# Issuing the rope's row swaps from ScalarE into a tile of their own, in a fused hybrid decoder block

## The chip, the cores and the metric

The kernel runs on one core of a Trainium2 chip. The metric is the device time of one launch in microseconds (us). An engine is named as in the profile: PE is TensorE (PEld its weight loads), DVE is VectorE, ACT is ScalarE, POOL is GpSimd, SP is SyncE, whose queue issues nearly all DMAs.

## The reference, cut to what matters

One decoder layer over 2048 tokens of 1024 channels: an adaptive RMSNorm, one input projection into queries (8 heads of 64), keys and values (2 heads) and a gated convolution group, sliding-window attention with rotary positions, an output projection, a gated MLP of 2816 channels with a convolution, and a last RMSNorm, all in float32. The changed part is the rotary step (rope):

```python
def rope(x, positions):
    ...
    x1, x2 = xf[..., :half], xf[..., half:]
    out = jnp.concatenate([x1 * cos - x2 * sin, x2 * cos + x1 * sin], axis=-1)
    return out.astype(x.dtype)
...
q = rope(q.reshape(bsz, s, N_Q_HEADS, HEAD_DIM), positions)
k = rope(k.reshape(bsz, s, N_KV_HEADS, HEAD_DIM), positions)
```

Each half of a head (32 channels) needs the other half of the same head.

## The kernel before, in words

Channels lie on partitions and tokens along the free axis. The mixer (the first 850 us or so) goes through four quarters q = 0 to 3 of 512 tokens. In a quarter the projection is computed in steps of one 128-channel tile: 24 matmuls of 128x512 into a PSUM tile `ps`, of which there are two. For q > 0 the order is k (tile 4), q0, q1, v (tile 5), and then, as filler between attention pieces, q2, q3 and the twelve convolution tiles. The attention goes in eight pieces g (4 blocks of 128 tokens for each key head): `scores(g)` (matmuls `sc<-kt,qs`), softmax, `trans(g)` (transposes into `tr`, then the copies `pt`), `pv(g)`. scores(0) to scores(3) need the roped k, q0 and q1; later ones need q2 and q3. Each scores(g) has two halves: the first reads the `qs` tile of q0 (or q2), the second that of q1 (or q3). scores(0) stands after q2 and two eighths of q3 in quarters 1 to 3, and inside the second convolution tile in quarter 0, where the six tiles of k, q and v are done in `start` with PSUM banks of their own.

A roped tile comes about so: ACT copies `ps` to `rq` with a bias (L496, `evac_bias`); four DMAs of 32x512 (64 KB) from SP, L503, copy `rq` into a tile `sq` with the two 32-row halves of each head exchanged; DVE multiplies `rq` by the cosines `cs[:, 0]` (L504) and `sq` by the signed sines `cs[:, 1]` (L505) and adds them into `rq` (L506); ACT copies halves of `rq` to the rounded high parts (L337 and L534, into `kt` for k, four copies, or `qs` for q, two), and DVE takes the low parts (L338, L535). L504 writes `rq`, which the four DMAs read, so it waits for the last of them.

The tile `sq` has two buffers. They also hold the squares of the norm statistics (L323 and L324, one for each of the eight `xr` rows that end the quarter before), so a swap waits until the squares that were there have been added up. The order on each engine is made by a scheduler that plays the program through with a timeline of its own; matmuls keep the order in which they are written. Around the rope in quarters 1 to 3 the eight rows of the last quarter's output are finished: SP loads `xr` (L694), DVE adds to it (L695), SP stores it (L696), ACT squares it (L323).

Of the kernel before, what the change touches and what calls it, by code (L numbers as in the profile page):

```python
# [49 lines left out]
def body(tc, *a):  # L50
    nc = tc.nc
    with tc.tile_pool(name="cst", bufs=1) as cst, \
         tc.tile_pool(name="ps", bufs=1, space=PSUM) as pp, \
         tc.tile_pool(name="dr", bufs=1, space=DRAM) as dr:
        build(nc, tc, cst, pp, dr, *a)


def build(nc, tc, cst, pp, dr, xT, pos, pk_d, c_d, ada_d, w_in, w_o, w_up, w_dn, outT):
# [3 lines left out]
    dma = nc.sync.dma_start  # L62
# [18 lines left out]
    def aux_tile():  # L81
# [2 lines left out]

    TAGS = {'h': (1024, 8), 'y': (1024, 8), 'qs': (1024, 4), 'pp': (1024, 2), 'pt': (512, 6),
# [3 lines left out]

    where = {}  # L90
# [8 lines left out]
    def t(tag, shape=None, dt=F32):  # L99
        p, (n, bufs) = where[tag]  # L100
        return p.tile(shape or [128, n], dt, tag=tag, name=tag, bufs=bufs)
# [396 lines left out]

    def rope(raw, cs, mode=0):
        m = [pool if mode >> i & 1 else vec for i in range(3)]  # L500
        sw = t('sq')
        for i in range(4):
            dma(sw[32 * i:32 * i + 32], raw[32 * (i ^ 1):32 * (i ^ 1) + 32])  # L503
        m[0].tensor_tensor(out=raw, in0=raw, in1=cs[:, 0], op=ALU.mult)  # L504
        m[1].tensor_tensor(out=sw, in0=sw, in1=cs[:, 1], op=ALU.mult)  # L505
        m[2].tensor_tensor(out=raw, in0=raw, in1=sw, op=ALU.add)  # L506
        return raw
# [5 lines left out]
    class Attn:  # L513
# [14 lines left out]
        def k_out(self, p):  # L528
            kr = rope(evac_bias(p, 4, 'rq'), self.cs, RK[self.q])
            kt = self.kt = t('kt', [128, 2, 2, 640], F32R)  # L530
            for kv in range(2):
                own, oth = lohi[kv], lohi[1 - kv]
                split(kt[own, kv, 0, 128:640], kt[own, kv, 1, 128:640], kr[own], vec)
                act(kt[oth, kv, 0, 128:640], kr[own], AF.Copy)  # L534
                vec.tensor_tensor(out=kt[oth, kv, 1, 128:640], in0=kr[own], in1=kt[own, kv, 0, 128:640].bitcast(F32),  # L535
                                  op=ALU.subtract)
            if self.q > 0:
                fdma(kt[:, :, :, 0:128], prev_k[0])
            if self.q < NQ - 1:
                prev_k[0] = sb.tile([128, 2, 2, 128], F32R, tag="hk", name="hk")  # L540
                fdma(prev_k[0], kt[:, :, :, 512:640])

        def q_out(self, j):
            def f(p):
                qr = rope(evac_bias(p, j, 'rq'), self.cs, RQ[self.q][j])
                qt = self.qs[j] = t('qs', [128, 2, 512], F32R)
                for hh in range(2):
                    own, oth = lohi[hh], lohi[1 - hh]
                    split(qt[own, hh], qt[oth, hh], qr[own], pool if SQ[self.q][j] else vec)
            return f  # L550
# [759 lines left out]
```

## Time and profile before

| what | value |
|---|---|
| median of 3 runs | 2240.99 us (2240.96 to 2241.58) |
| profiled execution | 2238.82 us, span 2237.0 us |
| PE, DVE, ACT, POOL busy | 92%, 71%, 44%, 24% of the span |
| mean granted clock of PE | 0.967 of full speed |

The span is that of the program's instructions; the execution is 1.8 us longer than it, and the median 2.2 us longer than the profiled execution.

### The profile page before, as it was taken

Reading aid. Unit: us, or ns where it says so; the run is one execution under the profiler, and the core shown is the slowest. Engines: PE = TensorE matmul, PEld = TensorE weight load, DVE = VectorE, ACT = ScalarE, POOL = GpSimd, SP = SyncE. Lnnn points to the kernel's source line nnn. Section 1 sums busy time; section 2 is a strip of 40 time slices with the busy share of each in tenths; the row PEclk is TensorE's granted clock in tenths of the full one; section 3 lists DMA queues with packets and bytes.
Section 4 is the critical chain, followed back from the end, with each engine's and each line's share of the span. In section 5 each row is a group of like instructions: output and inputs, shape, how many; then the busy total and the mean of one; then the engine's idle time right before and its main releaser. Section 6 shows DMA issues by size and latency. Waiting matters only on the chain.

```text
span 2237.0 us, 26087 instructions
## 1 busy us (share of the span) xinstructions
PE 2058.7 (92%) x8914; PEld 1646.0 (74%) x8914; DVE 1592.7 (71%) x2589; ACT 985.9 (44%) x1719; POOL 532.9 (24%) x306
## 2 busy tenths in 40 slices
PE   4877968988998997999999998999999999999996
PEld 3765757766777775877887877787788888878874
DVE  8897548747854759888888868758877777654454
ACT  3564435435533534544444434544544444434341
POOL 5264410000000001323323323423232323212220
PEclk7998989999999998999999999999999999999997
DMA  7674776677667556545345566665433232256662
GB/s 284 208 257 144 268 252 244 231 255 249 213 215 241 171 177 228 181 149 178 138 172 171 188 202 191 195 198 178 156 104 109 90 112 100 99 175 201 190 203 97
DMA packets 164918, 414.80 MB, mean 185 GB/s; under 512 B 19248, under 2 KB 23344, under 8 KB 152240
## 3 DMA queue, kind: packets, MB, share of 16 engines
q1 hardware_dynamic: 164640, 413.02, 54.5%
q8 instruction: 70, 1.15, 0.2%
q14 instruction: 64, 0.52, 0.1%
q10 hardware_dynamic: 144, 0.11, 0.0%
HBM read 304.52 MB, written 100.93 MB: 181 GB/s over the span
## 4 chain that ended last, share of the span: by engine, by line
PE 44%; DVE 4%; DMA 3%; issue 1%; ACT 1%; SPq 0%; POOL 0%; DVEq 0%; ACTq 0%; POOLq 0%
PE ps L67 21%; PE sc L67 12%; PE tr L67 7%; PE aux L67 2%; PE pv L67 1%; DVE op L338 1%; DMA wr<-tt 1%; DVE S L759 1%; DMA u<-x1d 0%; DMA wr<-w_dn 0%; ACT op L337 0%; DMA tb<-x1d 0%; DMA y<-x1d 0%; DVE x L1118 0%; DMA f<-u 0%
## 5 line engine op out<-in xcount | busy, mean ns | idle before, releaser
L338 POOL TENSOR_TENSOR op<-wr,op 128x512 fp32r<-128x512 f32 (+1 forms) x123 | 240.3, 1954 | 1221.6 <-DVE o L338 585.9
L67 PE MATMUL ps<-h,w 128*128 128x512 f32 x1632 | 425.6, 411 | 37.1 <-ACT rq L496 15.1
L67 PE MATMUL ps<-S,op 128*128 128x512 f32 x1584 | 389.9, 399 | 21.8 <-ACT op L337 11.5
L67 PEld LDWEIGHTS ps<-h,w 128*128 128x128 f32 x1632 | 311.3, 195 | 115.6 <-ACT rq L496 17.7
L67 PEld LDWEIGHTS ps<-S,op 128*128 128x128 f32 x1584 | 299.1, 189 | 98.8 <-ACT op L337 14.7
L337 ACT ACTIVATE op<-wr 128x1024 fp32r<-128x1024 f32 (+1 forms) x229 | 205.1, 896 | 254.6 <-PE sc L67 85.2
L338 DVE TENSOR_TENSOR op<-wr,op 128x1024 fp32r<-128x1024 f32 x106 | 140.4, 1327 | 135.8 <-ACT op L337 135.8
L1007 DVE SCALAR_TENSOR_TENSOR u<-G,pk,u 128x512 f32<-128x512 f32 x176 | 156.5, 891 | 34.2 <-ACT u L1004 32.6
L67 PE MATMUL sc<-S,op 128*128 128x512 f32 x528 | 131.0, 397 | 0.0
L67 PE MATMUL ps<-S,o 128*128 128x512 f32 x528 | 130.4, 395 | 0.0
L67 PE MATMUL tr<-S,op 128*128 128x512 f32 x528 | 130.3, 395 | 0.0
L67 PE MATMUL sc<-S,o 128*128 128x512 f32 x528 | 130.3, 395 | 0.0
L67 PE MATMUL ps<-op 128*128 128x512 f32 x462 | 120.0, 394 | 9.1 <-DVE op L338 4.8
L67 PE MATMUL sc<-op 128*128 128x512 f32 x462 | 118.4, 392 | 0.0
L67 PEld LDWEIGHTS sc<-S,op 128*128 128x128 f32 x528 | 99.8, 189 | 24.3
L67 PEld LDWEIGHTS sc<-S,o 128*128 128x128 f32 x528 | 99.1, 188 | 24.1
L67 PEld LDWEIGHTS tr<-S,op 128*128 128x128 f32 x528 | 99.1, 188 | 24.1
L67 PEld LDWEIGHTS ps<-S,o 128*128 128x128 f32 x528 | 99.0, 188 | 24.0
L67 PEld LDWEIGHTS ps<-op 128*128 128x128 f32 x462 | 86.6, 188 | 29.5 <-DVE op L338 5.6
L1004 ACT ACTIVATE u<-G,pk 128x512 f32<-128x512 f32 x88 | 71.4, 812 | 82.4 <-DVE G L988 80.7
L338 POOL TENSOR_TENSOR w<-wr,w 128x1024 fp32r<-128x1024 f32 x28 | 74.3, 2662 | 137.3 <-ACT w L337 116.3
L337 ACT ACTIVATE op<-ta 128x512 fp32r<-128x512 f32 x132 | 81.0, 624 | 57.6 <-PE ps L67 51.8
(315 smaller groups left out, 3533.6 us busy)
## 6 DMA issues: line engine op xcount, KB each, us to landing
w<-wd SPq DMA_DIRECT2D x72, 1024.0 KB, 5.9
wr<-w_up SPq DMA_DIRECT2D x86, 512.0 KB, 3.3
wd<-w SPq DMA_DIRECT2D x26, 1024.0 KB, 5.4
fs<-u SPq DMA_DIRECT2D x88, 256.0 KB, 2.1
wr<-fs SPq DMA_DIRECT2D x88, 256.0 KB, 2.9
wr<-tt SPq DMA_DIRECT2D x88, 256.0 KB, 3.3
f<-u SPq DMA_DIRECT2D x66, 256.0 KB, 2.0
wr<-f SPq DMA_DIRECT2D x66, 256.0 KB, 2.9
```

The lines of the kernel that those rows point to most:

```text
L67: i = nc.tensor.matmul(*a, **k)
L337: act(hi, src, AF.Copy)
L338: return lo_eng.tensor_tensor(out=lo, in0=src, in1=hi.bitcast(F32), op=ALU.subtract)
L759: vec.scalar_tensor_tensor(out=o[:, L], in0=src, scalar=bias, in1=o[:, W].bitcast(F32), op0=ALU.add, op1=ALU.subtract)
L1004: act(u, G[:, 2:], AF.Identity, scale=fwh[:, 2 * NFF + j:2 * NFF + j + 1], bias=fwh[:, 3 * NFF + j:3 * NFF + j + 1])
L1007: vec.scalar_tensor_tensor(out=u, in0=G[:, i:i + T], scalar=fwh[:, i * NFF + j:i * NFF + j + 1], in1=u, op0=ALU.mult, op1=ALU.add)
```

## The change

Three lines differ. The swapped halves go to a new tile `sw` with one buffer, not to one of the two buffers of `sq`, and the four DMAs are issued by ACT's queue, not by SP's.

```diff
-            'rq': (512, 5), 'hb': (512, 1), 'cv': (512, 2), 'cz': (514, 2), 'xr': (512, 2),
+            'rq': (512, 5), 'hb': (512, 1), 'sw': (512, 1), 'cv': (512, 2), 'cz': (514, 2), 'xr': (512, 2),
...
     def rope(raw, cs, mode=0):
...
-        sw = t('sq')
+        sw = t('sw')
         for i in range(4):
-            dma(sw[32 * i:32 * i + 32], raw[32 * (i ^ 1):32 * (i ^ 1) + 32])
+            nc.scalar.dma_start(sw[32 * i:32 * i + 32], raw[32 * (i ^ 1):32 * (i ^ 1) + 32])
```

There are 20 ropes (five in each quarter), so 80 DMAs change their queue. The order of PE's instructions stays as it was, and so do its PSUM banks; the scheduler reorders the others, mostly within the mixer.

On ACT, at the start of quarter 1, the rows before are these (`rq_2102` is k, `rq_2155` q0, `rq_2201` q1, `rq_2247` v, `rq_2280` q2):

```order
L496 ACTIVATE rq_2102<-ps_2077,pk_69 128x512
L337 ACTIVATE w_2218<-wr_2216 128x1024
L323 ACTIVATE sq_1982<-xr_1978 128x512
L496 ACTIVATE rq_2155<-ps_2130,pk_69 128x512
L337 ACTIVATE w_2251<-wr_2249 128x1024
L323 ACTIVATE sq_2051<-xr_2047 128x512
L496 ACTIVATE rq_2201<-ps_2176,pk_69 128x512
L337 ACTIVATE w_2297<-wr_2295 128x1024
L496 ACTIVATE rq_2247<-ps_2222,pk_69 128x512
L323 ACTIVATE sq_2058<-xr_2054 128x512
L496 ACTIVATE rq_2280<-ps_2255,pk_69 128x512
L337 ACTIVATE kt_2112<-rq_2102 64x512
```

With the change the same place on ACT reads so, from the copy of q0 on:

```order
L496 ACTIVATE rq_2155<-ps_2130,pk_69 128x512
L337 ACTIVATE w_2251<-wr_2249 128x1024
L323 ACTIVATE sq_2051<-xr_2047 128x512
L337 ACTIVATE kt_2112<-rq_2102 64x512
L534 ACTIVATE kt_2112<-rq_2102 64x512
L337 ACTIVATE kt_2112<-rq_2102 64x512
L534 ACTIVATE kt_2112<-rq_2102 64x512
L503 DMA sw_2157<-rq_2155 32x512 x4
L496 ACTIVATE rq_2201<-ps_2176,pk_69 128x512
L337 ACTIVATE w_2297<-wr_2295 128x1024
L496 ACTIVATE rq_2247<-ps_2222,pk_69 128x512
L323 ACTIVATE sq_2058<-xr_2054 128x512
```

The copies of k, which stood behind all five evacuations, now stand ahead of that of q1, with the four issues of q0's swap behind them; after these rows come the copies of q0, then the swap of q1, the evacuation of q2, the copies of q1 and the swap of q2. On DVE, L506 of k stands behind L695 of the seventh `xr` row and L506 of q0 behind L695 of the eighth.

On ACT in quarter 0, ahead of the first exponentials, these rows now stand (`rq_573` is q1, `rq_590` is q2):

```order
L337 ACTIVATE qs_568<-rq_558 64x512 x2
L503 DMA sw_575<-rq_573 32x512 x4
L337 ACTIVATE w_854<-wr_852 128x1024
L496 ACTIVATE cv_771<-ps_746,pk_69 128x512
L337 ACTIVATE w_968<-wr_966 128x1024
L337 ACTIVATE qs_583<-rq_573 64x512 x2
L503 DMA sw_592<-rq_590 32x512 x4
L596 ACT_TABLE_LOAD
```

Before, the copies of all four q tiles stood ahead of `cv_771`, and `w_968` behind the exponentials. On DVE in quarter 0 the rope of q1 now reads so (`sc_791` is the first half of scores(0)):

```order
L504 TENSOR_TENSOR rq_573<-rq_573,cs_523 128x512
L505 TENSOR_TENSOR sw_575<-sw_575,cs_523 128x512
L274 TENSOR_TENSOR g1_104<-g1_104,pk_69 128x2
L589 ISA pp_786,mx_787<-sc_791,mask_88 128x128
L589 ISA mx_787 128x1
...
L506 TENSOR_TENSOR rq_573<-rq_573,sw_575 128x512
```

Before, all of q1's rope stood 20 rows ahead of these maxima; now its last addition stands behind two of them (the rows left out are the second maximum), and q2's and q3's ropes behind the softmax of scores(0).

## Rows read from the trace of the kernel before

**Rows 1.** The page: span, and busy time of each engine.
```profile
span 2237.0 us, 26087 instructions
PE 2058.7 (92%) x8914; PEld 1646.0 (74%) x8914; DVE 1592.7 (71%) x2589; ACT 985.9 (44%) x1719; POOL 532.9 (24%) x306
```

**Rows 2.** Waits of PE, 70 to 850 us: total us, times, longest.
```profile
PE ps L67 <- ACT rq L496: 15.1, 6, 5.3
PE sc L67 <- DVE qs L338: 14.8, 5, 8.3
...
PE ps L67 <- DMA w<-wd: 1.8, 2, 1.1
```

**Rows 3.** Tile `sq`: duration min/median/max in ns, first and last start.
```profile
L503 SPq DMA_DIRECT2D sq<-rq x80: 507/588/1568, 77.2 to 719.8; - x80
...
L506 DVE TENSOR_TENSOR rq<-rq,sq x20: 675/691/693, 87.3 to 725.3; 128x512 f32<-128x512 f32 x20
...
DMA to landing us min/median/max: 1.9/4.6/7.4
```

**Rows 4.** Line L503, 309 to 313.5 us: issue to landing of six swaps.
```profile
DMA to landing us min/median/max: 1.9/2.1/2.8
```

**Rows 5.** Line L503, 498 to 502 us: issue to landing of four swaps.
```profile
DMA to landing us min/median/max: 6.2/6.9/7.4
```

**Rows 6.** Timeline of PE, quarter 1: start, duration, instructions, idle before.
```profile
291.39 5.86 PE L67 MATMUL ps<-h,w 128*128 128x512 f32 x24 [0.78 <-ACT rq L496]
...
313.60 1.51 PE L67 MATMUL sc<-kt,qs 128*128 128x256 f32 x4 [8.31 <-DVE qs L338]
320.55 0.79 PE L67 MATMUL sc<-kt,qs 128*128 128x256 f32 x2 [5.43 <-DVE qs L338]
322.00 0.80 PE L67 MATMUL sc<-kt,qs 128*128 128x256 f32 x2 [0.65 <-DVE qs L338]
```

**Rows 7.** Timeline of SP's queue, quarter 1.
```profile
298.50 7.32 SPq L503 DMA_DIRECT2D sq<-rq  x8
```

**Rows 8.** Timeline of ACT, quarter 1.
```profile
275.87 0.69 ACT L496 ACTIVATE rq<-ps,pk 128x512 f32<-128x512 f32 x1 [0.41 <-PE ps L67]
277.65 1.06 ACT L337 ACTIVATE w<-wr 128x1024 fp32r<-128x1024 f32 x1 [1.10 <-DMA wr<-w_in]
...
287.90 0.63 ACT L323 ACTIVATE sq<-xr 128x512 f32<-128x512 f32 x1 [2.25 <-DVE xr L695]
...
309.38 0.63 ACT L337 ACTIVATE kt<-rq 64x512 fp32r<-64x512 f32 x1 [4.77 <-DVE rq L506]
```

**Rows 9.** Timeline of DVE, quarter 1: the seventh and eighth `xr` row.
```profile
287.06 0.75 DVE L695 SCALAR_TENSOR_TENSOR xr<-pv,g,xr 128x512 f32<-128x512 f32 x1 [2.21 <-DMA xr<-xT]
...
297.32 0.75 DVE L695 SCALAR_TENSOR_TENSOR xr<-ps,g,xr 128x512 f32<-128x512 f32 x1 [8.07 <-PE ps L67]
```

**Rows 10.** Timeline of ACT, quarter 2.
```profile
490.84 0.63 ACT L323 ACTIVATE sq<-xr 128x512 f32<-128x512 f32 x1 [1.97 <-DVE xr L695]
```

**Rows 11.** Timeline of DVE, quarter 2: low parts of q1.
```profile
514.43 1.41 DVE L338 TENSOR_TENSOR qs<-rq,qs 64x512 fp32r<-64x512 f32 x2 [0.70 <-ACT qs L337]
```

**Rows 12.** Timeline of ACT, quarter 3.
```profile
688.76 0.63 ACT L323 ACTIVATE sq<-xr 128x512 f32<-128x512 f32 x1 [2.80 <-DVE xr L695]
...
714.20 0.51 ACT L596 ACTIVATE pp<-pp,nm 128x256 f32<-128x256 f32 x1 [1.44 <-DVE nm L592]
```

**Rows 13.** Timeline of PE, quarter 3: scores(0).
```profile
711.83 1.11 PE L67 MATMUL sc<-kt,qs 128*128 128x256 f32 x8
```

**Rows 14.** Timeline of PE, quarter 0.
```profile
110.44 2.90 PE L67 MATMUL ps<-h,w 128*128 128x512 f32 x6 [2.81 <-DVE yc L661]
113.14 1.15 PE L67 MATMUL sc<-kt,qs 128*128 128x128 f32 x8
```

**Rows 15.** Windows: length, busy us (count) of PE, PEld, DVE, ACT, POOL, clock, DMA share, GB/s.
```profile
130.00:240.00 110.00, 84.46 (x355) 64.08 (x354) 87.51 (x186) 54.91 (x126) 56.12 (x35) 0.88 0.53 177
...
489.00:492.00 3.00, 3.00 (x7) 2.40 (x8) 1.26 (x3) 0.63 (x1) 0.00 (x0) 0.50 0.99 309
492.00:495.00 3.00, 3.00 (x14) 2.39 (x13) 0.20 (x1) 0.00 (x0) 0.00 (x0) 0.95 0.88 290
```

## The prediction

> **What bounds the kernel now.** I read the page first: PE is busy for 2058.7 of 2237.0 us [rows 1], so a change off PE can win no more than PE's idle time, and only where the rope is what PE waits for. The waits of PE over the mixer say where: its scores matmuls wait 14.8 us in five places for the low parts of a roped query, and its projection matmuls 15.1 us for ACT's evacuation of a PSUM tile [rows 2]. For loads of kept weights they wait 1.8 us [rows 2]. Then the timelines: the rope's waits lie nearly all in quarter 1, where PE stands still for 8.31, 5.43 and 0.65 us ahead of scores(0) [rows 6], 14.4 us in all. In quarter 2 the low parts of q1 are done at 515.84 [rows 11], just when PE wants them, and in quarter 3 all eight scores matmuls run in one piece at 711.83 [rows 13]. In quarter 0, too, they run in one piece, at 113.14 [rows 14].
>
> The cause in quarter 1 is SP's order. ACT has evacuated k at 276.56 [rows 8], but SP issues the swaps of k and q0 at 298.50 [rows 7], 22 us later, behind the store of the last `xr` row.
>
> **The price of one rope on ACT's queue.** Four issues take 4 x 0.588 = 2.35 us [rows 3] if ACT issues as fast as SP, and ACT can do nothing else meanwhile. A swap lands 1.9 to 7.4 us after its issue starts, median 4.6 [rows 3]. The nearest to a free queue are the six at 309 us, 1.9 to 2.8 with a median of 2.1 [rows 4]; those behind weight loads took 6.2 to 7.4 [rows 5]. No row shows a swap on a queue of its own beside full DMA engines. Counted from the end of the last issue (0.59 us less), the bounds are 1.3 and 6.8; I take 1.9, near the free end, because the swap no longer stands behind the loads of its own queue, and call it a. Then three DVE operations of 0.69 us, 2.0 in all [rows 3], then the high copies, 0.63 each [rows 8] and about 0.65 with the gap: 2.6 for k, 1.3 for a query. With one buffer the next swap is issued only after L506, and by ACT's order after those copies. So the ropes form a chain: from L506 of k to L506 of q0 it takes 2.6 + 2.35 + 1.9 + 2.0 = 8.85 us, and on to that of q1 1.3 + 2.35 + 1.9 + 2.0 = 7.55.
>
> **Quarter 1.** k's swap is issued behind a weight copy that ends at 278.7 [rows 8], so it lands about 278.7 + 2.35 + 1.9 = 283. But L506 of k stands behind L695 at 287.06 [rows 9], so it ends near 288.5. The copies of k run from 288.5 (after L323 at 287.90 [rows 8]) to 291.1 and the issues of q0's swap to 293.5. Only then comes q1's evacuation, to 294.2; before, it had ended at 291.39 for the next step to start [rows 6], so PE loses 2.8 us there. v takes 5.9 us more, its evacuation ends at 300.8. L506 of q0 waits for L695 at 297.32 [rows 9] and ends at 298.8; its copies stand behind v's evacuation and L323 and end at 302.7; q1's swap is issued by 305.1, lands at 307.0; PE reaches scores(0) at about 308; DVE takes its two maxima and then does q1's rope by 311.2; copies and low parts let the last matmuls start near 313. Before, they started at 322.00 [rows 6]. **Gain 9 us.** Bounds: at most 14.4 - 2.8 = 11.6; and 8.3 if a is 4.0, since the two `xr` rows hide most of the later landings.
>
> **Quarter 2.** Three of k's four issues stand behind L323, which ends at 491.47 [rows 10]: 491.47 + 1.76 + 1.9 + 2.0 = 497.1 for L506 of k, 506.0 for q0, 513.5 for q1, and 2.1 more for the low parts (L338 pair of 1.41 after 0.70 [rows 11]) is 515.6, against 515.84 now. **Nothing**, and 6.3 us lost if a is 4.0, since three landings lie on the chain.
>
> **Quarter 3.** The same sum from 689.39 [rows 12]: 695.05, 703.9, 711.45, low parts at 713.55. PE asks for the last of them about 712.6, three quarters into its 1.11 us [rows 13]: 1 us. Then the evacuation and the four issues of q2 stand ahead of the first exponential, which moves from 714.20 [rows 12] to about 717, and the rope of q3 behind it by about as much; what follows on PE has little slack. **Loss 2 us**, 8.3 if a is 4.0, none at best.
>
> **Quarter 0.** ACT issues five groups of 2.35 us between 77 and 135 us, 11.8 us in all: the upper bound if every one is on the path. The first stands ahead of the copies of the cosine tables, the second ahead of the copy that frees PE's first convolution tile. Both delay PE before 110 us, where it waits 2.81 us for DVE in any case [rows 14]: this hides them, and costs 2.35 to 4.7 if that wait is gone. The third carries q1, whose L506 now stands behind two maxima of scores(0): the second half waits at least for 0.69 + 1.3 = 2.0 us, where the halves ran on without a gap [rows 14]. The fourth stands ahead of the first exponentials, the fifth ahead of the first `pt` copy, 2.35 each. 2.0 + 2.35 + 2.35 = 6.7; some of the fifth hides behind softmax work, so I take **a loss of 6 us**, bounds 2 and 11.8. A wait of 5 us can also lower PE's clock: after the 5 us before 489 the granted clock was 0.50 (the 1.2 GHz level) and PE did 7 matmuls in 3 us against 14 in the next three [rows 15], 1.5 us lost; this is inside the upper bound.
>
> **SP** loses 80 x 0.588 = 47 us of issues [rows 3]. That is worth at most the 1.8 us that PE waits for its loads [rows 2]; POOL's and ACT's weight splits keep their sources. I take 0. The moved tiles cost nothing: the same operations on other addresses.
>
> **The sum**: 6 - 9 + 0 + 2 = -1 us against the profiled execution's 2238.82; with the 2.2 us by which the median lies above it, 2240. A difference under 0.2% (4.5 us) can't be told from no change.
>
> **The rivals.**
>
> *Swaps land no sooner on ACT's queue* (slower). a stays at the median, 4.6 - 0.59 = 4.0. Then each serial chain pays 2.1 us per landing: quarter 0 +8, quarter 1 -8.3, quarter 2 +6.3, quarter 3 +8.3, sum +14: 2255. It decides from a = 2.65 on, since the sum rises by about 7 us for each us of a. For it: the DMA engines are 88 to 99% busy around 490 [rows 15]. Against: swaps with little queued ahead landed in 2.1 [rows 4]. The Trainium skill, DMA: Bandwidth & Descriptors, section Issuing engines are not separate DMA queues, says that DMAs of all issuing engines run on the same 16 DMA engines and interleave, and that a second issuer saves only issue time. Read strictly that is this rival, with 2255; no row here shows a swap issued by ACT. Chance 0.23.
>
> *Quarter 1 keeps most of its stall* (slower): the change doesn't do what it says where it counts. L506 of k and q0 still stand behind L695, which waits for loads of `xr` [rows 9]. Should the eighth row come 6 us later than 297.32, since SP's order around it changes as well, the gain is 3, and the sum +5: 2246. For it: these loads wait for stores to land. Against: SP is free of swaps there. Chance 0.10.
>
> *Quarter 0 absorbs its delays* (faster). Between 130 and 240 us PE is idle for 110 - 84.46 = 25.5 us [rows 15]. If a delay at 114 us only fills such gaps, the sum is -7: 2234. It decides where quarter 0 costs under 2.5. Against: DVE is busy for 87.5 of these 110 us, and PE waits there for the very softmax that is late. Chance 0.25.
>
> **How the numbers follow.** My forecast, within 0.2%, has 0.42. Faster 0.25, slower 0.23 + 0.10 = 0.33. The range is 2231 to 2255: down to the faster case with 3 us for a quarter 1 that wins up to the 11.6 of its bound, up to the first rival.
>
> **What would show it.** Swaps in ACT's queue with a landing of about 2.5 us from issue (a = 1.9); in quarter 1, L506 of k near 288 and of q0 near 299, q1's evacuation near 294, scores(0) done near 313 counted from the same point of PE's program; in quarters 2 and 3 a wait of PE for `qs` of 0 and 1 us; in quarter 0 one of 2 to 5 us in the middle of scores(0), with the first exponentials some 5 us late. The prediction is wrong if ACT issues much more slowly than SP, if a is above 2.65, or if the reordered softmax of quarter 0 shifts by more than 10 us.

## The result, and the profile after

The changed kernel takes 2259.59 us in the median (2255.63 to 2270.0, 6 runs), the kernel before 2241.28 (2240.07 to 2249.12, 6 runs) on the same chip: a ratio of 1.0083, 95% interval 1.0060 to 1.0107, or 18.6 us more. That is slower by more than 0.2%, and just outside the range of 2231 to 2255, on the side of the first rival. The profiled execution took 2255.63 us, 16.8 more than that of the kernel before.

The page of the kernel after, to set beside [rows 1]:

```profile
span 2253.7 us, 26074 instructions
PE 2069.8 (92%) x8914; PEld 1653.7 (73%) x8914; DVE 1586.7 (70%) x2589; ACT 985.3 (44%) x1719; POOL 535.2 (24%) x306
```

Each engine runs as many instructions as before. Of 16.7 us more span PE's busy time takes 11.1, for the same 8914 matmuls, while its mean granted clock fell from 0.967 to 0.963. Part of it is paid behind the long waits: after 6.34 and 5.35 us of standing still (the timeline of PE below) the granted clock was 0.50, the lower of its two levels (1.2 GHz). The windows give length, busy us (count) of PE, PEld, DVE, ACT, POOL, clock, DMA share and GB/s:

```profile
118.70:121.70 3.00, 2.93 (x8) 2.42 (x9) 1.52 (x7) 0.15 (x1) 0.00 (x0) 0.50 1.00 392
306.70:309.70 3.00, 2.96 (x7) 2.41 (x8) 0.00 (x0) 0.93 (x1) 1.99 (x1) 0.50 0.97 253
```

So the 24 matmuls at 306.74 took 7.71 us, where the same 24 took 5.86 before [rows 6]. The waits of PE over the mixer (70 to 850 us; total us, times, longest) beside [rows 2]:

```profile
PE ps L67 <- ACT rq L496: 22.5, 8, 5.3
...
PE sc L67 <- DVE qs L338: 15.7, 6, 6.3
```

The 14.8 us for roped queries, which the change was to take away, are still there, and the wait for ACT's evacuations has grown by 7.4. The tile `sw`, beside [rows 3]:

```profile
L503 ACTq DMA_DIRECT2D sw<-rq x80: 514/606/2107, 77.2 to 737.2; - x80
...
  DVE rq L504: 49.1, 14
...
DMA to landing us min/median/max: 1.9/4.9/8.3
```

A swap lands 4.9 us after its issue starts, against 4.6 before: **no sooner on ACT's queue**. DVE's L504 waits 49.1 us for swaps in 14 places, where it waited 31.6 us in 11 before. Where a swap is issued matters little, and when it is issued much. The line L503 from 284 to 292 us, among weight loads, and then from 520 to 530 us:

```profile
DMA to landing us min/median/max: 4.9/6.5/8.3
```

```profile
DMA to landing us min/median/max: 1.9/2.0/2.4
```

The DMA engines were busy all the time in the first of these stretches (share 1.01) and about half of the second (0.48):

```profile
284.00:292.00 8.00, 6.26 (x27) 4.74 (x26) 1.44 (x2) 3.21 (x4) 4.79 (x2) 1.00 1.01 413
520.00:530.00 10.00, 6.61 (x31) 4.91 (x30) 6.00 (x17) 3.06 (x6) 0.00 (x0) 1.00 0.48 152
```

The timeline of DVE in quarters 0 and 1 (start, duration, instruction, idle before):

```profile
111.75 1.21 DVE L168 CUSTOM_DVE_ANT_0 wr<-wr,cr 128x1024 f32<-128x1024 f32 x1
...
112.89 0.68 DVE L504 TENSOR_TENSOR rq<-rq,cs 128x512 f32<-128x512 f32 x1
...
114.58 2.72 DVE L506 TENSOR_TENSOR rq<-rq,sw 128x512 f32<-128x512 f32 x1
...
300.35 0.69 DVE L504 TENSOR_TENSOR rq<-rq,cs 128x512 f32<-128x512 f32 x1 [4.73 <-DMA sw<-rq]
...
302.22 0.68 DVE L506 TENSOR_TENSOR rq<-rq,sw 128x512 f32<-128x512 f32 x1
...
311.29 0.69 DVE L504 TENSOR_TENSOR rq<-rq,cs 128x512 f32<-128x512 f32 x1 [4.90 <-DMA sw<-rq]
...
312.50 0.74 DVE L695 SCALAR_TENSOR_TENSOR xr<-ps,g,xr 128x512 f32<-128x512 f32 x1
313.16 0.68 DVE L506 TENSOR_TENSOR rq<-rq,sw 128x512 f32<-128x512 f32 x1
```

The first three rows are of quarter 0: q1's rope there. In quarter 1 DVE stands still for k's swap and then for that of q0. The eighth `xr` row (312.50) now stands behind a swap's landing and not, as forecast, the rope behind the row. ACT in quarters 0, 1 and 2:

```profile
104.97 0.64 ACT L337 ACTIVATE qs<-rq 64x512 fp32r<-64x512 f32 x1 [6.33 <-DVE rq L506]
105.14 0.51 ACTq L503 DMA_DIRECT2D sw<-rq  x1
...
288.15 5.03 ACTq L503 DMA_DIRECT2D sw<-rq  x4
...
302.94 0.63 ACT L337 ACTIVATE kt<-rq 64x512 fp32r<-64x512 f32 x1
303.10 0.51 ACTq L503 DMA_DIRECT2D sw<-rq  x1
...
305.35 0.60 ACTq L503 DMA_DIRECT2D sw<-rq  x1
306.00 0.69 ACT L496 ACTIVATE rq<-ps,pk 128x512 f32<-128x512 f32 x1 [0.49 <-issue]
...
507.04 0.63 ACT L337 ACTIVATE kt<-rq 64x512 fp32r<-64x512 f32 x1 [1.86 <-DVE rq L506]
...
518.81 0.63 ACT L337 ACTIVATE qs<-rq 64x512 fp32r<-64x512 f32 x1 [8.03 <-DVE rq L506]
```

The evacuation of q1 at 306.00 stands behind k's copies and the four issues, and PE waits for it. The timeline of PE, from quarters 0 to 3:

```profile
111.84 0.56 PE L67 MATMUL sc<-kt,qs 128*128 128x128 f32 x4
118.74 1.41 PE L67 MATMUL sc<-kt,qs 128*128 128x128 f32 x4 [6.34 <-DVE qs L338]
...
306.74 7.71 PE L67 MATMUL ps<-h,w 128*128 128x512 f32 x24 [5.35 <-ACT rq L496]
...
322.32 0.63 PE L67 MATMUL sc<-kt,qs 128*128 128x256 f32 x4
327.74 1.51 PE L67 MATMUL sc<-kt,qs 128*128 128x256 f32 x4 [4.79 <-DVE qs L338]
...
526.57 0.50 PE L67 MATMUL sc<-kt,qs 128*128 128x256 f32 x2 [2.12 <-DVE qs L338]
...
727.82 0.50 PE L67 MATMUL sc<-kt,qs 128*128 128x256 f32 x2 [1.99 <-DVE qs L338]
```

Before, scores(0) had no such wait in quarters 0 and 3 [rows 13, 14]. In quarter 1 the start at 306.74 answers to 291.39 of [rows 6]: 15.3 us later, 9.4 of them inherited from quarter 0.

PE runs its matmuls in the same order in both traces, so the start of the n-th matmul can be compared. Taken at the ends of the quarters:

| matmul that started before at | later after | the quarter's term |
|---|---|---|
| 274.96 us (quarter 0 done) | 9.4 us | +9.4 |
| 469.98 us (quarter 1 done) | 6.6 us | -2.9 |
| 680.04 us (quarter 2 done) | 11.9 us | +5.3 |
| 840.00 us (quarter 3 done) | 15.5 us | +3.6 |
| 2199.38 us | 16.6 us | +1.1 for the rest |

These are single executions. In the variant below that changes only quarters 2 and 3, every engine's program is that of the kernel before until 490 us, and yet its terms for quarters 0 and 1 are -2.4 and +4.5: a term of less than about 5 us can't be told from none in this way.

### The profile page after: what moved, and what is told of

Its sections match the earlier page's. It is cut to its first block, busy times and chain, and to the rows that moved or that the text cites. A ratio compares the mean times of both kernels' runs of the same rounds, so it can differ in the third digit from the quotient of the medians.

```text
span 2253.7 us, 26074 instructions
## 1 busy us (share of the span) xinstructions
PE 2069.8 (92%) x8914; PEld 1653.7 (73%) x8914; DVE 1586.7 (70%) x2589; ACT 985.3 (44%) x1719; POOL 535.2 (24%) x306
## 3 DMA queue, kind: packets, MB, share of 16 engines
q10 hardware_dynamic: 3984, 5.35, 0.9%
## 4 chain that ended last, share of the span: by engine, by line
PE 45%; DVE 4%; DMA 2%; ACT 1%; issue 1%; SPq 0%; POOL 0%; DVEq 0%; ACTq 0%
PE ps L67 21%; PE sc L67 13%; PE tr L67 7%; PE aux L67 2%; PE pv L67 1%; DVE op L338 1%; DMA wr<-tt 1%; DVE S L759 1%; ACT op L337 0%; DMA wr<-f 0%; DMA y<-x1d 0%; DMA u<-x1d 0%; DVE x L1118 0%; ACT S L337 0%; DVE y L1118 0%
## 5 line engine op out<-in xcount | busy, mean ns | idle before, releaser
L67 PE MATMUL ps<-h,w 128*128 128x512 f32 x1632 | 433.0, 416 | 42.9 <-ACT rq L496 22.5
L67 PE MATMUL ps<-S,op 128*128 128x512 f32 x1584 | 389.8, 399 | 21.0 <-ACT op L337 10.9
L67 PEld LDWEIGHTS ps<-h,w 128*128 128x128 f32 x1632 | 316.3, 198 | 124.0 <-ACT rq L496 26.0
L338 DVE TENSOR_TENSOR op<-wr,op 128x1024 fp32r<-128x1024 f32 x106 | 134.9, 1275 | 138.2 <-ACT op L337 136.6
L67 PE MATMUL tr<-op 128*128 128x512 f32 x396 | 102.3, 393 | 4.5 <-DVE op L338 4.5
```

The lines of the kernel that those rows point to most:

```text
L67: i = nc.tensor.matmul(*a, **k)
L338: return lo_eng.tensor_tensor(out=lo, in0=src, in1=hi.bitcast(F32), op=ALU.subtract)
```

## The experiments

**Theory A**: the swap's landing, about 4.3 us after its last issue, is paid again in each link of the chain that the one buffer makes. **Theory B** (rival): ACT's queue is the cost, since issues and waiting copies stand ahead of PE's evacuations. Differences in us are the ratio of the runs times the median of before in the same comparison (2241.3 to 2244.1). The scheduler orders each variant anew, so a few us between two variants can be order alone; no run separates the two. Diffs are against the changed kernel unless said otherwise.

**One tile, SP's queue.**

```diff
-            nc.scalar.dma_start(sw[32 * i:32 * i + 32], raw[32 * (i ^ 1):32 * (i ^ 1) + 32])
+            dma(sw[32 * i:32 * i + 32], raw[32 * (i ^ 1):32 * (i ^ 1) + 32])
```

> The swaps go back to SP's queue, but keep the tile of their own with its one buffer. Theory A (a swap's landing of about 4.3 us after its issues, paid in series because the one buffer lets only one swap be under way): quarters 0, 2 and 3 pay the landings as in the changed kernel and quarter 1 keeps the 14 us of stalls of the kernel before, so 2255 to 2265. Theory B (ACT's queue: issues and waiting copies stand ahead of PE's evacuations): ACT is as free as before, PE's waits for ACT's rq are back near 15 us, and the time is 2240 to 2246.

2245.07 us, ratio 1.0003 (0.9989 to 1.0017), +0.7 us. That is theory B's number; by it the one buffer alone costs nothing. The runs with two tiles, below, show that it costs a great deal and what it is set off against here.

**The shared tile, ACT's queue.**

```diff
-        sw = t('sw')
+        sw = t('sq')
```

The variant does not declare `sw` either.

> The swaps stay on ACT's queue, but in the tile sq with its two buffers as before. If the single buffer is what makes the landings add up (theory A), a query's swap is issued before the L506 ahead of it has run, one landing of 4.3 us per quarter and more is hidden, and the time is 2240 to 2248. If ACT's queue is the cost (theory B), ACT still issues 80 times and the time stays at 2254 to 2262. Sharing sq with the squares can add waits of its own of 1 to 3 us.

2252.31 us, 1.0038 (1.0022 to 1.0054), +8.5: between the two. The timeline of ACT in its quarter 1:

```profile
307.71 0.63 ACT L323 ACTIVATE sq<-xr 128x512 f32<-128x512 f32 x1 [0.79 <-DVE xr L695]
307.79 10.17 ACTq L503 DMA_DIRECT2D sq<-rq  x8
318.00 0.69 ACT L496 ACTIVATE rq<-ps,pk 128x512 f32<-128x512 f32 x1 [9.66 <-DVE sq L505]
```

Here k's swap is issued at 307.8, right behind the last square, though no store of SP stands ahead of it. So it was not SP's order that made it late in the kernel before [rows 7] but the tile shared with the squares; the run with two tiles on SP's queue, below, shows the same from the other side.

**Copies by ACT, no transfer.**

```diff
-            nc.scalar.dma_start(sw[32 * i:32 * i + 32], raw[32 * (i ^ 1):32 * (i ^ 1) + 32])
+            act(sw[32 * i:32 * i + 32], raw[32 * (i ^ 1):32 * (i ^ 1) + 32], AF.Copy)
```

> The four swap transfers of a rope become four copies of 32 partitions by ACT, into the same tile with one buffer. ACT is held for about as long as by the four issues (4 x 0.6 = 2.4 us), but nothing has to land. Theory A: the terms of the sum at a = 0 are quarter 0 +4, quarter 1 -11, quarters 2 and 3 0: about 2233, range 2226 to 2241. Theory B (ACT held for 2.35 us per rope is the cost): 2254 to 2262, as the changed kernel.

2241.51 us, 0.9984 (0.9973 to 0.9996), -3.6, half a us above theory A's range. Its tile `sw`:

```profile
L503 ACT ACTIVATE sw<-rq x80: 625/629/634, 77.5 to 713.6; 32x512 f32<-32x512 f32 x80
```

ACT is held as long per copy (0.629 us) as an issue takes (0.606 above, in the median), the tile has one buffer as in the changed kernel, and the 18.6 us are gone: 22 us between the two, which the landing tells apart (and the order, which is made anew). For the changed kernel as a whole theory A holds and B alone does not. Quarter 0 is the exception: by the starts of the matmuls the copies, from which nothing has to land, still lose 6.9 us there, of the changed kernel's 9.4.

**The change in quarter 1 alone, in quarter 0 alone, in quarters 2 and 3 alone** (`self.q` is handed to `rope`; the diff is that of quarter 1, the others read `q == 0` and `q > 1`).

```diff
-        sw = t('sw')
+        sw = t('sw' if q == 1 else 'sq')
         for i in range(4):
-            nc.scalar.dma_start(sw[32 * i:32 * i + 32], raw[32 * (i ^ 1):32 * (i ^ 1) + 32])
+            (nc.scalar.dma_start if q == 1 else dma)(sw[32 * i:32 * i + 32], raw[32 * (i ^ 1):32 * (i ^ 1) + 32])
```

> Only quarter 1's five swaps are issued by ACT and use the tile of their own; the other fifteen go by SP and sq as before. If quarter 1's own net gain is what the changed kernel's trace shows from its start to its end (3 us), the time is 2237 to 2239. If its gain was cut by the 9 us of delay that quarter 0 handed it, the gain here is the 8.3 us of the sum at a = 4.0: 2231 to 2234. If the swap's price on ACT's queue leaves no gain where it counts: 2241 or more.

> ACT's queue and the tile of its own for the ropes of quarter 0 alone; the rest as before. Theory A by the changed kernel's trace: +9.4 us at the end of quarter 0, kept to the end, so +7 to +11 on the kernel before. The predicted term was +6. If the gaps of quarter 0 absorb the delays: within 2.

> ACT's queue and the tile of its own for the ropes of quarters 2 and 3 alone. By the changed kernel's trace +5.5 and +3.5: +9 us on the kernel before, 6 to 12; at a = 4.0 the prediction's own sum gives 6.3 + 8.3 = +14.6; with the 1.9 that I took it gives +2. With quarter 0 alone and quarter 1 alone (-5, measured) the three should add up to the +18.6 of the changed kernel, if the quarters' terms are independent.

Quarter 1: 2239.55 us, 0.9977 (0.9967 to 0.9987), -5.2. Quarter 0: 2257.12, 1.0053 (1.0032 to 1.0074), +11.9, a little over theory A's number. Quarters 2 and 3: 2260.17, 1.0073 (1.0054 to 1.0093), +16.4. Together +23.1, beside +18.6 (13.4 to 24.0) for the whole change: the terms add up within the error. Quarter 1 gains, by an amount between the two that I expected, and the other three lose over five times as much. Quarters 2 and 3 lose more than the changed kernel's trace says (+9), and about the 14.6 of the prediction's own formula at a = 4.0; by the starts of the matmuls in this variant's own trace, 6.2 and 9.5. The timeline of PE in that variant, quarters 2 and 3:

```profile
519.63 0.50 PE L67 MATMUL sc<-kt,qs 128*128 128x256 f32 x2 [2.12 <-DVE qs L338]
...
728.14 1.52 PE L67 MATMUL sc<-kt,qs 128*128 128x256 f32 x4 [5.74 <-DVE qs L338]
```

**Copies in quarter 1 alone, and in quarters 1 to 3** (transfers by SP into `sq` elsewhere; the diff is that of quarter 1, the other reads `if q`).

```diff
-        sw = t('sw')
+        sw = t('sw' if q == 1 else 'sq')
         for i in range(4):
-            nc.scalar.dma_start(sw[32 * i:32 * i + 32], raw[32 * (i ^ 1):32 * (i ^ 1) + 32])
+            if q == 1:
+                act(sw[32 * i:32 * i + 32], raw[32 * (i ^ 1):32 * (i ^ 1) + 32], AF.Copy)
+            else:
+                dma(sw[32 * i:32 * i + 32], raw[32 * (i ^ 1):32 * (i ^ 1) + 32])
```

> Only in quarter 1 are the swaps four copies by ACT each, in the tile of their own; in quarters 0, 2 and 3 they are transfers on SP's queue in sq, as before. Theory A (the landing is the loss, ACT's share of a swap is cheap where DVE and PE have other work): quarter 1 wins the 12.7 us that its stretch won in the trace with copies everywhere, quarter 0 loses nothing: 12 us under the kernel before, 2227 to 2235. Theory B (ACT held is the cost): quarter 1 wins no more than the 4.6 us that it won with its swaps on ACT's queue, 4 to 6 us under the kernel before.

> Copies by ACT in quarters 1, 2 and 3, transfers on SP's queue in sq in quarter 0. By the terms of the trace with copies everywhere (quarter 0 +7, quarter 1 -13, quarters 2 and 3 -2 together) leaving out quarter 0 gives -15: 2224 to 2232 beside 2241 to 2244. If quarter 1's gain there came only because quarter 0 was late, as its loads were no later: -8, 2233 to 2236.

Quarter 1 alone: 2224.73 us, 0.9927 (0.9910 to 0.9945), -16.4: more than was expected, more than the 11.6 that the prediction gave as the most that quarter 1 could win, and a version that beats both kernels. Quarters 1 to 3: 2227.14, 0.9938 (0.9919 to 0.9958), -13.9, as the first case said: in quarters 2 and 3 the copies bring nothing.

**Two tiles.** `hb`, idle most of the mixer, serves in turn with `sw`, and no square uses either.

```diff
-        sw = t('sw')
+        sw = t(next(alt))
...
-    RK = (0, 0, 0, 0)
+    RK, alt = (0, 0, 0, 0), iter(('sw', 'hb') * 10)
```

> The swaps on ACT's queue as in the changed kernel, but in turn into the tile of their own and into hb, which lies idle nearly all the time: two buffers that no square uses. If the one buffer makes ACT's landings add up: half of the 18 us comes back or more, +2 to +8 us on the kernel before. If the landing of a swap on ACT's queue and its place in ACT's order are the loss in any case: +14 to +18. If the squares that share sq cost the variant with sq as much as its second buffer gave: less than +4.

2231.79 us, 0.9963 (0.9950 to 0.9977), -8.3. This is the change as it stands, on ACT's queue, with a second buffer: 27 us under the changed kernel. It is the third case, and lower than I had thought possible. ACT in its quarter 1:

```profile
283.89 4.78 ACTq L503 DMA_DIRECT2D hb<-rq  x4
...
291.10 5.03 ACTq L503 DMA_DIRECT2D sw<-rq  x4
...
298.37 0.63 ACT L337 ACTIVATE kt<-rq 64x512 fp32r<-64x512 f32 x1
```

The swap of q0 is issued 7 us ahead of the first copy of k, not behind it as at 302.94 and 303.10 above, so its landing passes beside k's.

**Two tiles, SP's queue** (the two-tile diff, with `dma` for `nc.scalar.dma_start`).

> The same two tiles in turn (the tile of its own and hb), with the swaps back on SP's queue. If what won with two tiles on ACT's queue (9.5 us under the kernel before) was quarter 1 freed from SP's order, quarter 1 keeps its stalls here and the time is that of the kernel before within 4 us. If it was that the swaps no longer share their tile with the squares, whatever queue they are on, the time is 5 to 12 us under the kernel before.

2227.31 us, 0.9923 (0.9908 to 0.9938), -17.3, more than the 5 to 12 that I gave: the queue was no part of the remedy. SP's timeline in its quarter 1:

```profile
281.01 4.21 SPq L503 DMA_DIRECT2D hb<-rq  x4
...
289.43 2.84 SPq L503 DMA_DIRECT2D sw<-rq  x4
```

SP itself issues k's swap at 281.0, where it did at 298.5 before [rows 7], and its scores(0) run in one piece:

```profile
310.25 1.11 PE L67 MATMUL sc<-kt,qs 128*128 128x256 f32 x8
```

**Copies by ACT into two tiles** (the two-tile diff, with `act` and `AF.Copy` as in the copies above).

> ACT's copies for every rope, into the two tiles in turn. With transfers the second tile won 17 us on SP's queue and 27 on ACT's. If the one tile costs that much because a landing of 4 to 5 us is paid again in each link of the chain, the copies, which have none, win little by a second tile: 0 to 6 us under the copies into one tile, 2231 to 2241 beside a kernel before of 2243. If it is the waiting for L505 and L506, which copies pay too, the second tile wins 10 us or more here: under 2230.

2226.46 us, 0.9938 (0.9923 to 0.9954), -13.9: 10 under the copies into one tile. So the second tile is worth something even where nothing lands, since the next swap then need not wait for L505 and L506. In us against the kernel before:

| | `sq`, shared with squares | one tile of its own | two tiles |
|---|---|---|---|
| transfers, SP | 0 | +0.7 | -17.3 |
| transfers, ACT | +8.5 | +18.6 | -8.3 |
| copies by ACT | not run | -3.6 | -13.9 |

Each entry carries an error of 3 to 4 us, and a difference between two of them one of about 5. Read across: sharing with the squares costs 17 us on either queue, and one tile in place of two costs 18 on SP, 27 on ACT and 10 for copies. Theory A's number for the first experiment failed because there the 17 and the 18 cancel. Read down: ACT's queue costs 8.5 and 9.0 with two buffers and 17.9 with one. A landing (transfers by ACT against copies by ACT) costs 22 us with one tile and 5.6 with two.

The starts of the matmuls say where, with the noise of some 5 us in each term that was found above:

| term in us | quarter 0 | quarter 1 | quarter 2 | quarter 3 |
|---|---|---|---|---|
| transfers, ACT, one tile (the changed kernel) | +9.4 | -2.9 | +5.3 | +3.6 |
| transfers, SP, one tile | +5.7 | -3.3 | +4.2 | +0.4 |
| transfers, SP, two tiles | +0.9 | -13.0 | -1.8 | -1.3 |
| copies by ACT, one tile | +6.9 | -12.7 | -2.5 | -0.2 |
| copies by ACT, two tiles | -1.9 | -12.3 | +0.5 | -0.6 |

Taking away the landing (first row against fourth) wins 9.8 and 7.7 us in quarters 1 and 2, and 2.5 in quarter 0. What quarter 0 loses comes with the one buffer, whether something lands or not: 8.8 us between the two rows of copies.

**Each copy made twice**, one tile.

```diff
-        for i in range(4):
-            nc.scalar.dma_start(sw[32 * i:32 * i + 32], raw[32 * (i ^ 1):32 * (i ^ 1) + 32])
+        for i in range(8):
+            act(sw[32 * (i % 4):32 * (i % 4) + 32], raw[32 * ((i % 4) ^ 1):32 * ((i % 4) ^ 1) + 32], AF.Copy)
```

> Copies by ACT for every rope, and each copy made twice: ACT is held for 5.0 us per rope in place of 2.5, and still nothing lands. It prices a microsecond of ACT's queue. Theory A: ACT's share lies on the same chain as the landing, at the 5 us per us that the landing cost (22 us between swaps as transfers and as copies, for 4.3 us): 2.5 x 5 = 12.5 us over the copies made once, +9 on the kernel before. Theory B: a held ACT costs more than a landing, since evacuations wait too: +16 us or more over the copies made once. If most of ACT's time is hidden: under 5 us.

2267.23 us, 1.0114 (1.0094 to 1.0135), +25.6, 29 over the copies made once. That is theory B's number, and A's assumption that a microsecond costs the same on both falls: 20 ropes x 2.5 = 50 us more of ACT cost 29, while 20 landings of 4.3 = 86 us cost 22. It does not price a held ACT alone, since the second copies also lengthen the chain by 2.5 us per link.

**GpSimd's copies in quarter 1.**

```diff
-        sw = t('sw')
+        sw = t('sw' if q == 1 else 'sq')
         for i in range(4):
-            nc.scalar.dma_start(sw[32 * i:32 * i + 32], raw[32 * (i ^ 1):32 * (i ^ 1) + 32])
+            (pool.tensor_copy if q == 1 else dma)(sw[32 * i:32 * i + 32], raw[32 * (i ^ 1):32 * (i ^ 1) + 32])
```

> As the variant with ACT's copies in quarter 1 alone, but GpSimd makes the copies. No row shows its copy of 32 x 512; if it takes 1 us or less each and ACT's 2.5 us per rope were on quarter 1's path, the gain grows from 16.6 to 18 to 21 us under the kernel before. If GpSimd takes 1.5 us or more each, or delays its weight splits, the gain falls to 8 to 14.

2235.02 us, 0.9954 (0.9939 to 0.9970), -10.3: 6 less than ACT's copies win there, with an error of about 5. The copies are in the median as short as ACT's, so the reason that I gave for a smaller gain (1.5 us or more each) falls. Line L503 in its trace, then POOL, DVE and PE at scores(0) of quarter 1:

```profile
L503 POOL COPY sw<-rq x20: 602/613/1512, 278.3 to 321.0; 32x512 f32<-32x512 f32 x20
...
298.35 3.29 POOL L503 COPY sw<-rq 32x512 f32<-32x512 f32 x4 [2.61 <-DVE rq L506]
...
305.31 0.42 DVE L589 CUSTOM_DVE_ANT_0 pp<-sc,mask 128x256 f32<-128x256 f32 x1 [4.14 <-PE sc L67]
...
306.01 0.69 DVE L504 TENSOR_TENSOR rq<-rq,cs 128x512 f32<-128x512 f32 x1
...
309.46 0.79 PE L67 MATMUL sc<-kt,qs 128*128 128x256 f32 x2 [4.18 <-DVE qs L338]
```

PE waits for no weight split of POOL's in this stretch. It waits 4.4 us for q1's rope: that swap is copied by 301.64, but DVE, which stands idle for 4.14 us meanwhile, takes it up only at 306.01, behind the first maxima of scores(0), whereas with ACT's copies scores(0) runs in one piece. So the trace puts most of the 6 us down to the order of DVE's rows, not to the copies.

**Two tiles on SP's queue, copies in quarter 1.**

> The two tiles in turn on SP's queue, with quarter 1's swaps as ACT's copies. Each alone is 17 us under the kernel before, and both take away the same stalls of quarter 1, so together no more than 17 to 20: 2223 to 2228 beside 2243. If the two tiles won elsewhere than in quarter 1: 22 us or more.

2228.17 us, 0.9938 (0.9925 to 0.9952), -13.9: no better than either alone, as it should be if both take away the same stalls of quarter 1. By the starts of the matmuls quarter 1 wins 12.3 us here, beside 13.0 with two tiles on SP's queue and 14.8 with its swaps as ACT's copies.

## Why the prediction was wrong

**The step that failed** is a term of the sum: a, the landing after the last issue. I took 1.9 us, "near the free end, because the swap no longer stands behind the loads of its own queue". It measured 4.9 - 0.6 = 4.3 in the median, and more where it counted: in quarter 1 DVE takes up k's swap 300.35 - 288.15 = 12.2 us after its first issue and q0's 311.29 - 303.10 = 8.2, where the sum had 2.35 + 1.9 = 4.25. The mechanism around it was right in quarters 1 to 3: the ropes of a quarter form a chain through one buffer, and the landing is paid in each link. From k's L506 to that of q0 I had 8.85 us; in quarter 1 it is 313.16 - 302.22 = 10.9, and in quarter 2 the first copies of k and q0 lie 518.81 - 507.04 = 11.8 apart. The prediction's sum rose by 15.3 us, to +14.3, as a went from 1.9 to 4.0, that is 7.3 per us; at 4.3 it gives -1 + 7.3 x 2.4 = +16.5, and 18.6 was measured. That these lie so close is in part luck: in the changed kernel's trace quarter 1 came out 5.4 us worse than the formula has it at a = 4.0 and quarter 3 4.7 us better, and the quarters alone add up to 23.1.

The first rival was this case. The Trainium skill, DMA: Bandwidth & Descriptors, section Issuing engines are not separate DMA queues, says that transfers of all issuing engines run on the same 16 DMA engines and interleave. The trace agrees: median landing 4.6 us on SP's queue and 4.9 on ACT's. I weighed it at 0.23 because a few swaps had landed in 2.1 [rows 4]. On ACT's queue, too, they land in 2.0 after 520 us and in 6.5 at 284: the rows of [rows 4] showed a quieter moment (a DMA share of 0.70 from 309 to 313.5 us of the kernel before, 0.84 from 498 to 502), not a short queue.

**Quarter 0**, predicted +6 (bounds 2 to 11.8): +11.9 alone, +9.4 in the changed kernel. The delays before 110 us were absorbed as forecast (the matmul at 110.44 starts 0.07 us earlier), so the third rival was right there, and only there; then scores(0) waited 6.34 us in its middle where I had 2 to 5. This was no landing: L504 of q1 starts at 112.89 right behind other work of DVE, with no wait for the swap. By the chain the swap had been issued only at 105.14, behind the first of q0's copies. So q1's rope stood behind a row of weight work (111.75); its L506 stood behind the two maxima, as forecast, and then took 2.72 us in place of 0.69, for which the trace names no reason. The copies by ACT, with one tile, lose 6.9 us here with nothing to land: in this quarter the chain through one buffer was the loss, and a only a small part of it.

**Quarter 1**, predicted -9: -5.2 alone, -2.9 in the changed kernel; at a = 4.0 the sum had -8.3, so even the rival was too hopeful. Two landings stand where I had counted on the two `xr` rows to hide them; the order of cause was the other way round. The second rival's condition came about by it: the eighth row is 312.50 - 297.32 - 9.4 = 5.8 us later [rows 9], because it stands behind the swap. The cause named for the stalls, SP's order, was wrong: the tile shared with the squares set it, as SP's own queue shows with two tiles. This cost the forecast nothing, since the change takes the swaps out of that tile too, but it hid that the tile alone, with two buffers, wins 17 us. And 11.6 us was no upper bound for quarter 1: the copies there won 16.4 (12.3 to 20.2).

**Quarters 2 and 3**, predicted 0 and +2: +16.4 together when alone, +5.3 and +3.6 in the changed kernel; the formula at a = 4.0 had 14.6, so alone they fit the sum with a larger a; in the changed kernel's trace they cost less.

**The price of an issue**, 0.588 us, was right in the median (0.606), and not where the DMA engines are busy all the time: four issues took 5.03 us at 288.15, not 2.35. That ACT can do nothing else meanwhile was too strict, as the last section shows. **SP's relief** of 47 us of issues was put at 0, and nothing shows a gain from it: with two tiles SP's queue is 9 us better than ACT's.

Open is how the 8.5 to 9 us that ACT's queue costs with two buffers divide among evacuations that come late, longer issues, and the order that the scheduler made of each variant.

## What to carry to other kernels

Before moving a small transfer to another engine's queue, ask what it waits for: its issuer's order, its buffer, or the DMA engines; the queue answers only the first, and here it was the second. A buffer of its own unties a transfer from its neighbours, but with a single one each landing is paid in series: here the second buffer was worth more than the whole change cost. Where a landing of several microseconds stands on a chain, a copy by an engine with time to spare can take its place, in the stretch where the chain is what PE waits for and not everywhere.

## What the runs showed of the hardware that was not expected

An issue on ACT's queue lies partly beside ACT's own work: the one at 303.10 starts while the copy of 302.94 to 303.57 still runs. An issue took 514 ns at the shortest, 606 in the median and 2107 at the longest, and the evacuation at 306.00 waited 0.49 us for nothing but the issues ahead of it. GpSimd copies 32x512 float32 across partitions in 613 ns in the median (602 to 1512), about as fast as ACT (629).
